# A bias table written in 16 shifted copies, and the scan's decay and angle operands made by ScalarE in pieces

## The chip, the cores and the metric

The kernel runs on one core of a Trainium2 chip. The metric is the device time of one execution in microseconds; the kernel before takes 1424.28 us, the median of three runs (1424.28 to 1425.12).

## The reference, cut to what matters

One decoder block with 256 tokens of width 2048, all in float32. A state-space branch and an attention branch both read the same normed input, are gated and added, and an MLP follows.

```python
mod = c_act @ w_ada[l] + b_ada[l]
...
h = rms_norm(x, norm_mix_g[l]) * (1.0 + sc1) + sh1
proj = h @ w_in[l]
u, q, k, v, ga, gb = jnp.split(proj, split_at, axis=-1)
y_ssm = s5_branch(u, ...)        # diagonal recurrence: 64 groups of 16 channels, 64 complex states
y_att = moba_attention(q, k, v, rel_bias)   # 8 heads, one block of 256 keys: causal softmax
...
merged = (jax.nn.sigmoid(ga) * (y_ssm @ w_proj_ssm[l])
          + jax.nn.sigmoid(gb) * (y_att @ w_proj_attn[l]))
x = x + g1 * (merged @ w_out[l])
h2 = rms_norm(x, norm_mlp_g[l]) * (1.0 + sc2) + sh2
x = x + g2 * (jnp.square(jax.nn.relu(h2 @ w_ff1[l])) @ w_ff2[l])
...
s_own = (jnp.einsum('hqd,hsd->hqs', qc, k_own) * scale
         + bias_table[:, t5_bucket(rel_own)])
s_own = jnp.where(rel_own[None] >= 0, s_own, NEG_INF)
```

The bias of a score depends on the distance of query and key alone (32 buckets, 8 heads). So the table that attention adds is, for each head, one row of 383 numbers that is read at another offset for each query.

## The kernel before, in words

**Weight tiles.** All large products run over one stream of weight tiles of 512 KB (128 x 1024). `load` starts a tile's DMA on SyncE's queue into `wraw` (7 buffers). `split` then makes two parts of it: ScalarE (ACT) casts the high part `whi` (L137) and VectorE (DVE) subtracts it to get the low part `wlo` (L139); each has 4 buffers. TensorE (PE) then runs 24 matmuls for the tile in `gemm_t` (L167 and L168 on `whi`, L169 on `wlo`) or 12 wider ones in `gemm_n` (L219 to L221). Where the text says "tile n", n counts the `wlo` instructions on DVE, in both kernels. A `gemm_t` sums into four banks `pt` of PSUM. Five banks are there for that, so the next product can start on one bank, and needs an evacuation of the last product's banks for each of the others. For the gates of the merge the evacuation is ACT's copy at L1030 into `ga` or `gb`.

**Lanes.** Between the tiles stand small jobs. One lane is the product with `w_ada`, whose tiles go through DVE alone (L275). One makes the state-space operands (`ssm_builds`): complex products `cc` on DVE (`cmul`, L528 to L530), 64 x 64 transposes `trv` (L565) and 128 small matmuls `rk` (L598), which read copies `tt` that ACT spreads (L588) and whose results DVE adds into `rt` (L604). One is attention, head by head: scores `sco` (L652, L653), the bias added by DVE (L655, L656), exponentials and scalings on ACT (L660 to L664), transposes `ptr` (L671) with ACT's copy L672, and values `pav` (L679, L680) with ACT's copy L682. Its scratch lies in columns 8 to 13 of `ga`, the tile that the second half of the first gate is evacuated to; that evacuation waits until the heads are done with the columns. The last lane is the scan.

**The scan.** The 256 tokens are four interleaved blocks b = 0 to 3. For each, `ssm_table` makes sine and cosine of 8 x 64 angles: DVE multiplies `cvec` by `g` (L724), ACT adds and takes off a large constant to round (L726, L727), DVE subtracts (L728), and ACT takes the sine, the absolute value and the sine again (L729, L730, L731). `ssm_in` then runs 32 small matmuls `vr` and `vi` (L745), makes the decay row `dk` on DVE (L747) and rotates the input (L749 to L754). `ssm_scan` is two scan instructions (L762) and six products (L766 to L771), and `ssm_ys` 48 matmuls (L783, L786) and ACT's copy L787.

**The bias.** `bias_prep` multiplies `rel_bias` by a one-hot matrix into 8 rows of 383 and has GpSimd's queue (POOL) write 32 copies of each to DRAM as `scr`. `bias_load` reads them back with four DMAs (L404), each for 32 partitions, so that every partition gets its row at its own offset (`tz`). Ahead of these on POOL's queue stand the 32 DMAs of `hop_in` (L704), which lay `u` out for the scan.

**Who sets the order.** The kernel is built with a planner that simulates the engines and so sets the order of each engine's queue. The text of the program gives the dependences and priorities. When an instruction is taken away, added, or moved to another engine, the planner can order much else in another way. On the chip each engine runs its queue in that order, and an instruction that waits holds all behind it.

Of the kernel before, what the change touches and what calls it, by code (L numbers as in the profile page):

```python
# [12 lines left out]
F32 = mybir.dt.float32  # L13
F32R = mybir.dt.float32r
I32 = mybir.dt.int32
AF = mybir.ActivationFunctionType
# [3 lines left out]
P = 128  # L20
S = 256
# [3 lines left out]
H = 8  # L25
# [13 lines left out]
VL = 383  # L39
# [35 lines left out]
class Kern:  # L75
# [307 lines left out]

    def bias_prep(self):
        nc, a = self.nc, self.a
        both = self.slot("SV", [P, 2, VL], name="oh")
        oh, vec = both[0:32, 0], both[0:H, 1]
        rb = self.cp.tile([32, H], F32, name="rb", tag="rb")
        nc.gpsimd.dma_start(oh, a["onehot"])
        nc.gpsimd.dma_start(rb, a["rel_bias"])  # L390
        p = self.aux("bv")
        with self.after(self.adac):
            nc.tensor.matmul(p[0:H, 0:VL], rb, oh, start=True, stop=True)
        nc.vector.tensor_copy(vec[:, 0:256], p[0:H, 0:256])
        nc.vector.memset(vec[:, 256:VL], NEG)
        self.scr = self.dr.tile([H, 32, VL], F32, name="scr")
        nc.gpsimd.dma_start(self.scr, vec[:, None, :].to_broadcast([H, 32, VL]))

    def bias_load(self):
        self.tz = self.slot("T", [P, H, S], name="tz")  # L400
        s = self.scr
        for g in range(4):
            src = bass.AP(tensor=s.tensor, offset=s.offset + 127 - 32 * g, ap=[[VL - 1, 32], [32 * VL, H], [1, S]])
            self.nc.gpsimd.dma_start(self.tz[32 * g:32 * g + 32], src)  # L404

    def exp_acc(self, x, name):
        nc, v = self.nc, self.nc.vector
# [313 lines left out]
    def ssm_table(self, b):  # L721
        nc, v = self.nc, self.nc.vector
        cs, sn = self.tbl[:, b % 2, 0], self.tbl[:, b % 2, 1]
        v.tensor_mul(sn.rearrange("p (k c) -> p k c", c=64), self.cvec[:, None, :].to_broadcast([P, 8, 64]),  # L724
                     self.g[:, b::4, None].to_broadcast([P, 8, 64]))
        nc.scalar.activation(cs, sn, AF.Identity, bias=self.mpos)  # L726
        nc.scalar.activation(cs, cs, AF.Identity, bias=self.mneg)  # L727
        v.tensor_sub(cs, sn, cs)  # L728
        nc.scalar.activation(sn, cs, AF.Sin, scale=SIN2PI)  # L729
        nc.scalar.activation(cs, cs, AF.Abs)  # L730
        nc.scalar.activation(cs, cs, AF.Sin, scale=-2.0 * math.pi, bias=self.hpi)  # L731
        return cs, sn

    def ssm_in(self, b, tabs):
        nc, v = self.nc, self.nc.vector
        if b + 1 < 4:
            tabs[b + 1] = self.ssm_table(b + 1)
        cs, sn = self.cur = tabs.pop(b)
        pr, pi = self.aux("vr"), self.aux("vi")
        for i, p in ((0, pr), (1, pi)):  # L740
            for k in range(8):
                c = slice(k * 64, (k + 1) * 64)
                for h in range(2):
                    q = slice(64 * h, 64 * h + 64)
                    nc.tensor.matmul(p[q, c], self.VT[q, i, 4 * k + b, :], self.U2[q, b, c], start=True, stop=True)  # L745
        wr, wi, t1, dk = [self.rw[:, i] for i in range(4)]
        v.tensor_mul(dk.rearrange("p (k c) -> p k c", c=64), self.cone[:, None, :].to_broadcast([P, 8, 64]),  # L747
                     self.mag4[:, b::4, None].to_broadcast([P, 8, 64]))
        v.tensor_mul(wr, pr, cs)  # L749
        v.tensor_mul(wi, pr, sn)  # L750
        v.tensor_mul(t1, pi, sn)
        v.tensor_add(wr, wr, t1)
        v.tensor_mul(t1, pi, cs)
        v.tensor_sub(wi, t1, wi)  # L754
# [516 lines left out]
```

## Time and profile before

| | us |
|---|---|
| median of 3 runs | 1424.28 |
| the profiled execution | 1427.57 |
| its span (first to last instruction) | 1425.8 |
| PE busy | 1375.2 |
| DVE busy | 1057.9 |
| ACT busy | 702.3 |
| POOL busy | 38.8 |

A profile is of one execution. Its span is 1.5 us over the median, and its time is 3.3 us over it. Times in rows of the trace count from the start of the span. A row of the timeline has the start, the busy time, engine, line, operation, result and sources, and in brackets the engine's idle time before it with what ended that. Instructions of one engine overlap at their ends, so the distance from one start to the next (here called the pitch) is shorter than a busy time.

### The profile page before, as it was taken

How to read it: one execution, taken by the hardware profiler on the slowest of the kernel's cores; microseconds unless marked ns; L12 is line 12 of the kernel's file. 1: busy time of each engine (PE TensorE's matmuls, PEld its weight loads, DVE VectorE, ACT ScalarE, POOL GpSimd, SP SyncE). 2: the span in 40 equal slices, each digit the busy share in tenths (PEclk: the TensorE clock that was granted, in tenths of full speed). 3: DMA queues.
4: the chain of work that ended last, by engine and by line, in shares of the span. 5: the costliest groups of instructions: out<-in, count | busy, mean ns of one | idle time of the engine just before them, and what ended most of it. 6: DMA issues, size and time to landing. Idle time of an engine off the chain costs nothing.

```text
span 1425.8 us, 23637 instructions
## 1 busy us (share of the span) xinstructions
PE 1375.2 (96%) x9370; PEld 1230.4 (86%) x9370; DVE 1057.9 (74%) x1507; ACT 702.3 (49%) x928; POOL 38.8 (3%) x89
## 2 busy tenths in 40 slices
PE   7789999999999999999899999999999999999996
PEld 5679899999999999988798888888888888888885
DVE  5588989976899788977686685778666555555676
ACT  4345353446645753444555555535364544635444
POOL 1000000310002200000000000000000000000000
PEclk9799999999999999999899999999999999999998
DMA  9999987777557988887497668677767666565561
GB/s 337 332 366 353 333 301 247 239 230 233 159 161 249 316 319 294 292 337 268 169 320 242 196 231 289 222 259 288 253 231 264 178 193 193 176 207 190 180 206 59
DMA packets 114382, 353.41 MB, mean 248 GB/s; under 512 B 12104, under 2 KB 12120, under 8 KB 114144
## 3 DMA queue, kind: packets, MB, share of 16 engines
q1 hardware_dynamic: 111408, 347.13, 71.3%
q0 software_dynamic: 2864, 4.78, 1.3%
q8 instruction: 73, 1.20, 0.3%
q14 instruction: 37, 0.30, 0.1%
HBM read 347.27 MB, written 2.49 MB: 245 GB/s over the span
## 4 chain that ended last, share of the span: by engine, by line
PE 85%; DVE 6%; DMA 4%; issue 2%; ACT 2%; SPq 0%; DVEq 0%; ACTq 0%
PE pw L195 15%; PE pn L221 11%; PE pn L219 11%; PE pn L220 11%; PE pt L169 9%; PE pt L167 9%; PE pt L168 9%; PE pw L197 8%; DVE wraw L275 2%; DMA wraw<-in_w_in_dram 2%; DVE wlo L139 2%; ACT whi L137 1%; DMA wraw<-in_w_proj_attn_dram 1%; PE ss L361 1%; PE rk L598 1%
## 5 line engine op out<-in xcount | busy, mean ns | idle before, releaser
L139 DVE TENSOR_TENSOR wlo<-wraw,whi 128x1024 fp32r<-128x1024 f32 x456 | 553.9, 1223 | 271.3 <-ACT whi L137 269.1
L137 ACT CAST whi<-wraw 128x1024 fp32r<-128x1024 f32 x456 | 474.8, 1050 | 567.4 <-PE pn L220 169.8
L195 PE MATMUL pw<-h2h,whi 128*128 128x512 f32 x960 | 332.8, 396 | 1.0 <-DVE part L1207 0.5
L197 PE MATMUL pw<-h2h,wlo 128*128 128x256 f32 x960 | 259.5, 280 | 1.7 <-DVE wlo L139 1.7
L167 PE MATMUL pt<-ah,whi 128*128 128x256 f32 x896 | 252.4, 289 | 8.0 <-ACT whi L137 5.1
L168 PE MATMUL pt<-ah,whi 128*128 128x256 f32 x896 | 251.8, 286 | 2.4 <-DVE ah L139 2.4
L169 PE MATMUL pt<-ah,wlo 128*128 128x256 f32 x896 | 241.9, 288 | 4.1 <-DVE wlo L139 3.9
L275 DVE SCALAR_TENSOR_TENSOR wraw<-wraw,cb 128x1024 f32<-128x1024 f32 x176 | 213.5, 1219 | 0.0
L195 PEld LDWEIGHTS pw<-h2h,whi 128*128 128x128 f32 x960 | 177.4, 188 | 39.4 <-DVE part L1207 0.8
L220 PE MATMUL pn<-whi,ff 128*128 128x512 f32 x512 | 199.4, 390 | 0.0
L219 PE MATMUL pn<-whi,ff 128*128 128x512 f32 x512 | 198.5, 390 | 0.0
L197 PEld LDWEIGHTS pw<-h2h,wlo 128*128 128x128 f32 x960 | 181.0, 189 | 6.9 <-DVE wlo L139 2.3
L221 PE MATMUL pn<-wlo,ff 128*128 128x512 f32 x512 | 182.7, 390 | 0.0
L167 PEld LDWEIGHTS pt<-ah,whi 128*128 128x128 f32 x896 | 173.0, 194 | 11.3 <-ACT whi L137 6.7
L168 PEld LDWEIGHTS pt<-ah,whi 128*128 128x128 f32 x896 | 173.7, 194 | 3.0 <-DVE ah L139 2.7
L169 PEld LDWEIGHTS pt<-ah,wlo 128*128 128x128 f32 x896 | 166.8, 194 | 5.9 <-DVE wlo L139 5.5
L219 PEld LDWEIGHTS pn<-whi,ff 128*128 128x128 f32 x512 | 96.1, 188 | 20.1 <-issue 0.2
L221 PEld LDWEIGHTS pn<-wlo,ff 128*128 128x128 f32 x512 | 96.1, 188 | 20.0
L220 PEld LDWEIGHTS pn<-whi,ff 128*128 128x128 f32 x512 | 96.1, 188 | 19.6
L219 PE MATMUL pn<-whi,mh 128*128 128x512 f32 x128 | 50.1, 392 | 0.0
L220 PE MATMUL pn<-whi,mh 128*128 128x512 f32 x128 | 49.9, 390 | 0.0
L221 PE MATMUL pn<-wlo,mh 128*128 128x512 f32 x128 | 46.2, 391 | 0.0
(337 smaller groups left out, 1570.5 us busy)
## 6 DMA issues: line engine op xcount, KB each, us to landing
wraw<-in_w_ff_dram SPq DMA_DIRECT2D x256, 512.0 KB, 4.8
wraw<-in_wat_dram SPq DMA_DIRECT2D x176, 512.0 KB, 5.8
wraw<-in_w_in_dram SPq DMA_DIRECT2D x128, 512.0 KB, 5.4
wraw<-in_w_out_dram SPq DMA_DIRECT2D x32, 512.0 KB, 6.5
wraw<-in_wan_dram SPq DMA_DIRECT2D x16, 512.0 KB, 8.9
wraw<-in_w_proj_attn_dram SPq DMA_DIRECT2D x16, 512.0 KB, 7.1
wraw<-in_w_proj_ssm_dram SPq DMA_DIRECT2D x16, 512.0 KB, 5.9
wraw<-in_w_glu_dram SPq DMA_DIRECT2D x8, 512.0 KB, 6.0
```

Of the source, the lines that this page charges most:

```text
L137: h = self.nc.scalar.copy(hi, src)
L139: s = self.nc.vector.tensor_sub(lo, src, hi.bitcast(F32))
L167: nc.tensor.matmul(o, hi[:, c], xh[:, kx, :], start=st, stop=False, skip_group_check=True)
L168: nc.tensor.matmul(o, hi[:, c], xl[:, kx, :], start=False, stop=False, skip_group_check=True)
L169: self.mm = nc.tensor.matmul(o, lo[:, c], xh[:, kx, :], start=False, stop=sp, skip_group_check=True)
L195: nc.tensor.matmul(banks[b], hi[:, c], x2[:, k0 + k].rearrange("p h s -> p (h s)"), start=i + k == 0, stop=False, skip_group_check=True)
L197: self.mm = nc.tensor.matmul(banks[b][:, 0:S], lo[:, c], x2[:, k0 + k, 0, :], start=False, stop=i == n - 1 and k == 1, skip_group_check=True)
L219: nc.tensor.matmul(o, xh[:, kx, tk], hi[:, c], start=q == 0, stop=False)
L220: nc.tensor.matmul(o, xl[:, kx, tk], hi[:, c], start=False, stop=False)
L221: self.mm = last = nc.tensor.matmul(o, xh[:, kx, tk], lo[:, c], start=False, stop=q == n - 1)
L275: v.scalar_tensor_tensor(w, w, 1.0, self.cb[:, (i % 2) * 1024:(i % 2 + 1) * 1024], op0=OP.mult, op1=OP.mult, accum_out=pc[:, i:i + 1])
L361: nc.tensor.matmul(p[:, 0:S], self.ones, jk[:, i, k], start=i + k == 0, stop=i + k == 6)
```

## The change

The diff has three edits. The first writes the bias table from 128 partitions: POOL copies `rel_bias` 16 times side by side, so one matmul gives 128 rows (16 copies of the 8 heads), which one DMA writes as they are. The table in DRAM has 16 copies for each head in place of 32, and `bias_load` reads it with eight DMAs of 16 partitions. The second replaces DVE's product at L724 by eight ACT instructions of 64 columns, each with one column of `g` as its scale. The third does the same for the decay row at L747. Over four blocks that is 8 DVE instructions fewer and 64 ACT instructions more.

```diff
-        both = self.slot("SV", [P, 2, VL], name="oh")
-        oh, vec = both[0:32, 0], both[0:H, 1]
+        both = self.slot("SV", [P, 2 * VL + P], name="oh")
+        oh, vec, rw = both[0:32, 0:VL], both[:, VL:2 * VL], both[0:32, 2 * VL:]
...
+        nc.gpsimd.tensor_copy(rw.rearrange("b (r h) -> b r h", h=H), rb[:, None, :].to_broadcast([32, P // H, H]))
...
-            nc.tensor.matmul(p[0:H, 0:VL], rb, oh, start=True, stop=True)
-        nc.vector.tensor_copy(vec[:, 0:256], p[0:H, 0:256])
+            nc.tensor.matmul(p[:, 0:VL], rw, oh, start=True, stop=True)
+        nc.vector.tensor_copy(vec[:, 0:256], p[:, 0:256])
         nc.vector.memset(vec[:, 256:VL], NEG)
-        self.scr = self.dr.tile([H, 32, VL], F32, name="scr")
-        nc.gpsimd.dma_start(self.scr, vec[:, None, :].to_broadcast([H, 32, VL]))
+        self.scr = self.dr.tile([P, VL], F32, name="scr")
+        nc.gpsimd.dma_start(self.scr, vec)
...
-        for g in range(4):
-            src = bass.AP(tensor=s.tensor, offset=s.offset + 127 - 32 * g, ap=[[VL - 1, 32], [32 * VL, H], [1, S]])
-            self.nc.gpsimd.dma_start(self.tz[32 * g:32 * g + 32], src)
+        for g in range(8):
+            src = bass.AP(tensor=s.tensor, offset=s.offset + 127 - 16 * g, ap=[[H * VL - 1, 16], [VL, H], [1, S]])
+            self.nc.gpsimd.dma_start(self.tz[16 * g:16 * g + 16], src)
...
-        v.tensor_mul(sn.rearrange("p (k c) -> p k c", c=64), self.cvec[:, None, :].to_broadcast([P, 8, 64]),
-                     self.g[:, b::4, None].to_broadcast([P, 8, 64]))
+        for k in range(8):
+            nc.scalar.activation(sn[:, 64 * k:64 * k + 64], self.cvec, AF.Copy,
+                                 scale=self.g[:, 4 * k + b:4 * k + b + 1])
...
-        v.tensor_mul(dk.rearrange("p (k c) -> p k c", c=64), self.cone[:, None, :].to_broadcast([P, 8, 64]),
-                     self.mag4[:, b::4, None].to_broadcast([P, 8, 64]))
+        for k in range(8):
+            nc.scalar.activation(dk[:, 64 * k:64 * k + 64], self.cone, AF.Copy,
+                                 scale=self.mag4[:, 4 * k + b:4 * k + b + 1])
```

With this the planner's order differs between about tile 54 and tile 112; from tile 113 on the queues are alike but for the line numbers (L724 becomes L726 on ACT, L726 to L731 become L728 to L733, L1030 becomes L1033, L598 becomes L599).

**First place: ACT at the start of the scan.** In the kernel before, ACT's queue has this where the tables of blocks 0 and 1 are made and the first gate's banks (`pt_...`) are evacuated:

```order
L137 CAST whi<-wraw 128x1024
L727 ACTIVATE tbl<-tbl,mneg 128x512 x2
L663 ACTIVATE ga<-ga,ast 128x128
L664 ACTIVATE ga<-ga,ast 128x256
L682 COPY yatt<-pav 128x256
L137 CAST whi<-wraw 128x1024
L729 ACT_TABLE_LOAD
L729 ACTIVATE tbl<-tbl 128x512
L1030 COPY ga<-pt_3376 128x512
L729 ACTIVATE tbl<-tbl 128x512
L730 ACTIVATE tbl<-tbl 128x512
L1030 COPY ga<-pt_3377 128x512
```

In the changed kernel, ACT's queue has this at the same place, from the first evacuation on:

```order
L1033 COPY ga<-pt_3384 128x512
L683 COPY yatt<-pav 128x256
L673 COPY ga<-ptr 128x384
L726 ACTIVATE tbl<-cvec,g 128x64 x4
L661 ACTIVATE ga,ast<-ga,ast 128x128
L726 ACTIVATE tbl<-cvec,g 128x64 x4
L662 ACTIVATE ga,ast<-ga,ast 128x256
L726 ACTIVATE tbl<-cvec,g 128x64 x8
L728 ACTIVATE tbl<-tbl,mpos 128x512
L1033 COPY ga<-pt_3381 128x512
L683 COPY yatt<-pav 128x256
L664 ACTIVATE ga<-ga,ast 128x128
```

Sixteen pieces now stand between the first and the second evacuation. The rest of both tables (another L728, two L729, a table load, two L731, two L732) stands ahead of the third, and a cast of a weight tile (tile 101's) only comes after all of it; before, casts, table steps and evacuations took turns.

**Second place: DVE at the same point.** Before, DVE's queue goes from the tables' subtraction over the `wlo` of tiles 99 and 100 to the first block's rotation and scan:

```order
L728 TENSOR_TENSOR tbl<-tbl 128x512 x2
L139 TENSOR_TENSOR wlo<-wraw,whi 128x1024 x2
L747 TENSOR_TENSOR rw<-cone,mag_308 128x512
L749 TENSOR_TENSOR rw<-vr,tbl 128x512
L750 TENSOR_TENSOR rw<-vr,tbl 128x512
L751 TENSOR_TENSOR rw<-vi,tbl 128x512
L752 TENSOR_TENSOR rw<-rw 128x512
L753 TENSOR_TENSOR rw<-vi,tbl 128x512
L762 SCALAR_TENSOR_TENSOR rw<-rw 128x512
```

In the changed kernel the subtraction stands behind the `wlo` of tiles 99 and 100, and DVE's queue goes on from it so:

```order
L730 TENSOR_TENSOR tbl<-tbl 128x512 x2
L139 TENSOR_TENSOR wlo<-wraw,whi 128x1024
L275 SCALAR_TENSOR_TENSOR wraw,pc<-wraw,cb 128x1024
L139 TENSOR_TENSOR wlo<-wraw,whi 128x1024 x2
L752 TENSOR_TENSOR rw<-vr,tbl 128x512
L753 TENSOR_TENSOR rw<-vr,tbl 128x512
L139 TENSOR_TENSOR wlo<-wraw,whi 128x1024
L754 TENSOR_TENSOR rw<-vi,tbl 128x512
```

The three `wlo` ahead of L752 are those of tiles 101, 102 and 103, so the first block's rotation has moved from ahead of tile 101 to behind tile 103.

**Third place: PE at the `rk` matmuls.** Before, they stand in the last product for the keys, in one row (all four blocks of 32):

```order
L598 MATMUL rk<-cc,tt 64x64 x2
L169 MATMUL pt_3049<-ah,wlo 128x256
L167 MATMUL pt_3049<-ah,whi 128x256
L168 MATMUL pt_3049<-ah,whi 128x256
L169 MATMUL pt_3049<-ah,wlo 128x256
L598 MATMUL rk<-cc,tt 64x64 x126
```

In the changed kernel they stand in the last tile of the product for `u`, some tiles earlier, and its matmuls stand between the two pairs of blocks:

```order
L599 MATMUL rk<-cc,tt 64x64 x62
L168 MATMUL pt_2587<-ah,whi 128x256
L169 MATMUL pt_2587<-ah,wlo 128x256
L167 MATMUL pt_2588<-ah,whi 128x256
L168 MATMUL pt_2588<-ah,whi 128x256
L169 MATMUL pt_2588<-ah,wlo 128x256
L167 MATMUL pt_2588<-ah,whi 128x256
L168 MATMUL pt_2588<-ah,whi 128x256
L169 MATMUL pt_2588<-ah,wlo 128x256
L599 MATMUL rk<-cc,tt 64x64 x64
```

The 126 in a row have become 62 and 64, and the DVE products `cc` that they read stand closer ahead of them.

## The prediction

> **What bounds the kernel now.** I read the page's busy shares first, then the chain that ended last:
>
> ```profile
> PE 1375.2 (96%) x9370; PEld 1230.4 (86%) x9370; DVE 1057.9 (74%) x1507; ACT 702.3 (49%) x928; POOL 38.8 (3%) x89
> PE 85%; DVE 6%; DMA 4%; issue 2%; ACT 2%; SPq 0%; DVEq 0%; ACTq 0%
> ```
>
> TensorE is busy 96% of the span and is 85% of the chain. All that the change touches lies beside TensorE, so it can only move the end by what it adds to, or takes from, TensorE's idle time. The order of the queues differs at about tiles 54 to 112, so the next view is TensorE's waits in 250 to 460 us, and after it the table of 20 us windows there (columns: sum, then busy time of PE, PEld, DVE, ACT, POOL):
>
> ```profile
> PE rk L598 <- issue: 2.1, 1, 2.1
> PE pt L169 <- DVE wlo L139: 1.4, 1, 1.4
> ...
> 360.00:380.00 20.00, 20.00 (x261) 19.70 (x260) 13.55 (x20) 15.85 (x26) 0.00 (x0) 1.00 0.44 133
> 380.00:400.00 20.00, 20.00 (x285) 19.60 (x284) 19.96 (x26) 9.05 (x11) 0.00 (x0) 1.00 0.71 227
> 400.00:420.00 20.00, 20.00 (x277) 19.67 (x279) 19.97 (x29) 9.88 (x12) 0.00 (x0) 1.00 0.34 111
> 420.00:440.00 20.00, 18.62 (x236) 18.15 (x232) 19.86 (x28) 7.72 (x10) 0.00 (x0) 1.00 0.63 200
> ```
>
> Only two waits are there to be won: 2.1 us in front of `rk` matmuls and 1.4 us at 431 us. But the windows show a second thing: from 380 to 440 us VectorE is full, 59.8 of 60 us. TensorE lives there on the lead that VectorE had when the scan began, and at 431 us the lead is used up. Whoever starts VectorE's stretch later, or lengthens it, makes TensorE wait; the stretch before it, 360 to 380, is where ScalarE is fullest (15.85 of 20).
>
> **The wait at `rk`.** Three pieces of the chain, then the window behind the wait (the column behind POOL is the granted clock) and the last of ScalarE's spread copies that these matmuls read:
>
> ```profile
> 277.72 5.74 PE rk L598 x191
> 283.46 2.05 issue
> 285.51 3.46 PE rk L598 x61
> ...
> 285.50:290.00 4.50, 4.49 (x70) 4.38 (x70) 1.60 (x4) 0.00 (x0) 3.22 (x7) 0.63 0.40 101
> ...
> 281.47 1.14 ACT L588 COPY tt<-cmp 128x512 f32<-128x512 f32 x2 [0.73 <-PE rk L598]
> ```
>
> The copies end at 282.6, so the 2.05 us from 283.46 are no wait for data ("issue" is a wait that the profile can't name). After it a matmul takes 3.46 / 61 = 0.057 us where it took 5.74 / 191 = 0.030, at a clock of 0.63: 61 x 0.027 = 1.6 us more. In all 3.65 us lie here. The changed order puts 62 and 64 matmuls in two places rather than 126 in one. I don't know whether the wait follows them: the gain is at most 3.65. In the new place VectorE's last `cc` product ends, by my count of its queue, about 0.6 us after TensorE gets there, and a spread copy of 1.14 / 2 = 0.57 us follows: 1.2 us, and 0.3 us for the second pair, so 1.5 us new. Taken: all of the old wait goes and 1.5 us comes, **-2.1 us**; ends -3.65 (nothing new) and +1.5 (old wait follows).
>
> The page "TensorE: Matmul & The Clock Gate" of the Trainium skill (its part on the clock gate) puts the fall of the clock behind an idle window of about 3.4 us; this row has it after 2.05 us, and the row decides. By the page the saving here would be 2.05 us alone.
>
> **The start of the scan, ScalarE.** ScalarE's timeline at the start of the scan before:
>
> ```profile
> 362.20 1.33 ACT L727 ACTIVATE tbl<-tbl,mneg 128x512 f32<-128x512 f32 x2
> 363.44 0.39 ACT L663 ACTIVATE ga<-ga,ast 128x128 f32<-128x128 f32 x1
> 363.74 0.49 ACT L664 ACTIVATE ga<-ga,ast 128x256 f32<-128x256 f32 x1
> 364.14 0.35 ACT L682 COPY yatt<-pav 128x256 f32<-128x256 f32 x1
> 364.55 1.05 ACT L137 CAST whi<-wraw 128x1024 fp32r<-128x1024 f32 x1
> 365.62 1.28 ACT L729 ACT_TABLE_LOAD   x1
> 366.91 0.63 ACT L729 ACTIVATE tbl<-tbl 128x512 f32<-128x512 f32 x1
> 367.45 0.57 ACT L1030 COPY ga<-pt 128x512 f32<-128x512 f32 x1
> 367.91 0.64 ACT L729 ACTIVATE tbl<-tbl 128x512 f32<-128x512 f32 x1
> ```
>
> By pitch: 128 columns 0.30, 256 columns 0.40, so a piece of 64 is estimated at 0.25 (ends 0.20, and 0.33 if columns don't count); 512 columns with a bias 0.62, without 0.54; an evacuation 0.46 to 0.5; the table load 1.28.
>
> Take the end of TensorE's tile 96 as zero. In the new order ScalarE's queue then goes: the first evacuation done at 1.4; the copy of a head's transposes done at 4.3 (it waits for TensorE); 16 pieces, 4.0, with two exponentials between them, 0.9 with their accumulator reads, to 9.2; L728 0.6; the second evacuation done at **10.3**; then a copy, two scalings, L728 and two L729, to 13.15; the load to 14.4; two L731 and two L732, 2.2, to 16.6; the third evacuation done at **17.1**; a sine, a copy, a sine to 18.7; the cast of tile 101 done at **19.65**.
>
> TensorE has tiles 97 to 100 ready but needs banks. By its queue it runs out at 8.3 and waits to 10.3, runs for 3.6 us on the next bank, and waits from 13.9 to 17.1: 2.0 + 3.2 = 5.2 us of idle that were not there before. The pieces make this: without their 4.0 us most of both goes.
>
> The Trainium skill's page "ScalarE: Activation LUTs" (row on a tight latency budget) gives about 0.3 us for an instruction and 0.83 ns for each element, 0.35 for a piece: it speaks against cutting into pieces, and by it the block is 5.6 us and the loss 1.6 larger. This trace's busy times agree (0.39 and 0.49), its pitch doesn't.
>
> **VectorE behind it.** It idles until the table is subtracted, and its full stretch begins with the `wlo` of tile 101 at 19.65. Its prices, from the full stretch:
>
> ```profile
> 429.25 1.21 DVE L762 TENSOR_TENSOR_SCAN rw<-rw 128x512 f32<-128x512 f32 x1
> 430.38 1.20 DVE L139 TENSOR_TENSOR wlo<-wraw,whi 128x1024 fp32r<-128x1024 f32 x1
> 431.50 1.22 DVE L275 SCALAR_TENSOR_TENSOR wraw<-wraw,cb 128x1024 f32<-128x1024 f32 x1
> 432.64 0.08 DVE L275 DVE_READ_ACCUMULATOR wraw<-wraw,cb 128x1 f32 x1
> 432.64 0.69 DVE L754 TENSOR_TENSOR rw<-rw 128x512 f32<-128x512 f32 x1
> 433.25 0.68 DVE L766 TENSOR_TENSOR sri<-rw,tbl 128x504 f32<-128x504 f32 x1
> 433.84 0.68 DVE L769 TENSOR_TENSOR sri<-rw,tbl 128x504 f32<-128x504 f32 x1
> ...
> L747 DVE TENSOR_TENSOR rw<-cone,mag 128x512 f32<-128x512 f32 x4 | 2.7, 686 | 0.3 <-PE pav L680 0.3
> L724 DVE TENSOR_TENSOR tbl<-cvec,g 128x512 f32<-128x512 f32 x4 | 2.6, 683 | 0.0
> ```
>
> A scan is 1.13, a `wlo` 1.14, an L275 1.14, a 512-wide product 0.60. From the `wlo` of tile 101 to that of tile 114 the new queue has 14 `wlo`, 4 L275, 7 scans and 43 products: 16.0 + 4.6 + 7.9 + 25.8 = 54.2 us, so tile 114's `wlo` ends at 19.65 + 54.2 + 0.5 for small gaps = 74.4. The eight products taken off VectorE (2.7 + 2.6 = 5.3 us) are left out already; two of them, for the first two tables, and the first L747 stood in a stretch where VectorE had idle time, and the others shorten the full one.
>
> TensorE's end of tile 96 and its wait for tile 114 before:
>
> ```profile
> 367.55 0.28 PE L169 MATMUL pt<-ah,wlo 128*128 128x256 f32 x1
> 431.63 0.39 PE L169 MATMUL pt<-ah,wlo 128*128 128x256 f32 x1 [1.38 <-DVE wlo L139]
> ...
> 297.12 0.22 PE sco L652 x2
> ```
>
> Between 367.7 and 431.6 it works 63.9 - 1.4 = 62.5 us. In the new order 12 small attention matmuls that stood ahead of tile 96 stand behind it, 12 x 0.22 = 2.6, with changes between forms some 3: 65.5. It waits 74.4 - 65.5 = 8.9 us in all there (5.2 for banks, the rest for `wlo`), against 1.4 before: **+7.5 us**. With pieces at 0.20 it is +6.7, at 0.33 +8.8; if attention's pieces fall better, the bank waits alone are left (below). A slower clock behind the bank waits lies in time that VectorE bounds; behind the last wait it may cost 0 (as after the 1.4 us) to 1.6 us: +0.5.
>
> **The bias and the decay row.**
>
> ```profile
> scr<-oh POOLq DMA_DIRECT2D x1, 383.0 KB, 10.3
> tz<-scr POOLq DMA_DIRECT2D x4, 256.0 KB, 4.8
> L404 POOL DMA_DIRECT2D tz<-scr x4 | 2.4, 597 | 0.0
> ```
>
> The write shrinks to 196 KB: 187 KB less, 0.5 us at the 337 GB/s of the page's first slices if the start is bound by transfers, 0 if not; taken -0.2. Four more issues on POOL are 2.4 us. By the new order `u` is evacuated some 4 us later, `hop_in` ends near 295 and the last `tz` issue near 300, landing near 305. The first head's bias stands four tiles later on VectorE, near 314, so 9 us cover it; without that cover the head, and through the evacuation of `ga` TensorE, would be late by what is missing. The decay pieces, 8 x 0.25 = 2 us on ScalarE for a block, lie where it works 9 of 20 us, and VectorE has five products ahead of the scan that reads them: nothing.
>
> **Sum.** -2.1 + 7.5 + 0.5 - 0.2 = +5.7 us. The profiled execution of 1427.57 would be 1433.3; that is 3.3 us over the median, and taken from the median the forecast is 1424.28 + 5.7 = **1430.0 us**. About 0.2%, 2.85 us, is what a measurement of this kernel can tell from no change.
>
> **Rivals.** *Faster, VectorE relieved.* If a piece's pitch is near 0.1, both evacuations come before TensorE runs out, VectorE's full stretch starts as early as before, its 5 or so products less remove the wait of 1.4 us, and the wait at `rk` goes: -1.4 - 3.65 - 0.5 = -5.5, 1418.8 us. For it: VectorE is the full engine and ScalarE half idle on average. Against it: no pitch in the rows is under 0.30, and ScalarE is not idle at 360 to 380. It decides if the second evacuation ends before 8.3. Chance 0.15.
>
> *No change.* VectorE makes good its late start, so that tile 114's `wlo` ends by 65.5 + 5.2 = 70.7 rather than 74.4 (the order lets it do 3.7 us more before tile 101 than I count). Then the bank waits are left: 5.2 - 1.4 - 3.65 = about 0, 1424.4 us. The bias edit gives nothing by itself in any case, since its cover is there in both. Chance 0.22.
>
> *Slower still.* The unnamed wait comes back in front of the new `rk` rows, with its slow clock, on top of the wait for `cc` (+1.5), and the clock falls behind the wait for tile 114 (+1.6): 7.5 + 1.5 + 1.6 = +10.6, 1434.9 us. For it: half of the 126 matmuls still stand in a row. Chance 0.15. The forecast itself has 0.48.
>
> **Range and chances.** From 1421.5, which leaves out most of the faster case, to 1437, above the slower case with pieces at 0.33. Faster by over 0.2% is the first rival, 0.15; within it is the second, 0.22; slower is the forecast and the third, 0.63.
>
> **What would show it.** In the changed profile: TensorE waits of about 5 us in all for the evacuation at L1033 and some 3 to 4 us for `wlo` between 360 and 445; ScalarE without a gap for about 14 us there; pieces with a pitch of 0.25; VectorE idle for about 10 us ahead of its full stretch; no 2 us of "issue" in `rk`. I am wrong if TensorE stays full from 360 to 420, or if a `rk` wait over 2 us is there.

## The result and the profile after

The changed kernel takes 1438.64 us (median of 4 runs, 1436.25 to 1440.31) against 1424.28 us of the kernel before: the ratio is 1.0083, 95% interval 1.0067 to 1.0099. It is slower, as forecast, but by 14.4 us where 5.7 were forecast, and the time lies 1.6 us above the range. One of the twelve runs of change_slow_lane, further below, took 1936.32 us at a granted clock of 0.653, and the ratios leave it out.

TensorE's waits between 250 and 470 us, in the changed kernel (what waits, for what: us in all, times, longest):

```profile
PE pt L167 <- ACT ga L1033: 5.2, 2, 3.3
PE rk L599 <- ACT tt L589: 3.3, 1, 3.3
PE pt L169 <- DVE wlo L139: 1.3, 1, 1.3
PE pt L167 <- DVE v L905: 1.1, 1, 1.1
PE ys L786 <- DVE sri L771: 0.7, 1, 0.7
```

The waits for the banks are there, two of them, 5.2 us in all. The old unnamed wait at `rk` has gone, and a wait of 3.3 us for ScalarE's spread copies has come. The wait for `v` was not in the forecast. Now the 20 us windows of the changed kernel, as those of before (busy time of PE, PEld, DVE, ACT, POOL, then the granted clock):

```profile
360.00:380.00 20.00, 16.28 (x129) 15.64 (x127) 6.28 (x14) 16.63 (x45) 0.00 (x0) 1.00 0.31 101
380.00:400.00 20.00, 18.53 (x220) 17.84 (x221) 15.07 (x19) 11.95 (x22) 0.00 (x0) 0.83 0.49 168
400.00:420.00 20.00, 19.33 (x274) 18.52 (x272) 19.52 (x27) 13.67 (x35) 0.00 (x0) 1.00 0.55 177
420.00:440.00 20.00, 19.61 (x277) 19.10 (x278) 19.43 (x27) 14.72 (x32) 0.00 (x0) 1.00 0.31 97
```

VectorE works 6.28 of the first 20 us, where it had 13.55 before, and its full stretch starts after 384. In the second window TensorE is busy 18.53 us but runs 220 matmuls where it ran 285: the clock is at 0.83 there.

Waits don't show what a slow clock costs. So the next table takes places at which TensorE has started the same matmuls in each kernel, and gives the time at which the next one starts (read from the traces, one profiled execution each; the kernels from the third column on are experiments, below).

| place | before | after | bias_only | rk_early | bias_slow_lane | change_slow_lane |
|---|---|---|---|---|---|---|
| A, the `pt` matmul behind the first modulation sums | 47.76 | 43.35 | 42.56 | 43.85 | 43.52 | 41.59 |
| B, ahead of the transposes `trv` and of `rk` | 238.77 | 234.36 | 233.73 | 235.84 | 233.94 | 232.88 |
| C, behind `rk` and the last `v` | 314.00 | 313.47 | 310.55 | 313.18 | 307.54 | 306.21 |
| E, the `wlo` of tile 114 | 431.63 | 441.94 | 435.86 | 431.64 | 425.17 | 426.04 |
| F, behind the scan | 485.21 | 495.25 | 489.73 | 486.99 | 477.94 | 479.13 |

Before against after: 4.4 us are won up to A, nothing changes from A to B (191.0 us in both), 3.9 are lost from B to C (75.2 against 79.1), 10.8 from C to E (117.6 against 128.5), and nothing that matters behind E. The traces show some of TensorE's matmuls in another order already from 52 us on, ahead of tile 54; by A to B that costs nothing. In all it is 10.0 us, and the two profiled executions (1437.97 and 1427.57 us) are 10.4 apart. The medians are 14.4 apart, because the profiled execution of before was 3.3 us over its median and that of after 0.7 under it.

### The profile page after: what moved, and what is told of

It is laid out like the page before. It is cut to its first block, busy times and chain, and to the rows that moved or that the text cites. A ratio compares the mean times of both kernels' runs of the same rounds, so it can differ in the third digit from the quotient of the medians.

```text
span 1436.2 us, 23699 instructions
## 1 busy us (share of the span) xinstructions
PE 1379.3 (96%) x9370; PEld 1231.6 (86%) x9370; DVE 1055.1 (73%) x1499; ACT 717.5 (50%) x992; POOL 40.8 (3%) x94
## 4 chain that ended last, share of the span: by engine, by line
PE 84%; DVE 7%; DMA 5%; ACT 3%; issue 1%; SPq 0%; DVEq 0%; ACTq 0%
PE pw L195 15%; PE pn L221 11%; PE pn L219 11%; PE pn L220 11%; PE pt L167 9%; PE pt L169 9%; PE pt L168 9%; PE pw L197 7%; DMA wraw<-in_w_in_dram 2%; DVE wlo L139 2%; DVE wraw L275 2%; ACT whi L137 1%; PE rk L599 1%; DMA wraw<-in_w_ff_dram 1%; PE ss L361 1%
## 5 line engine op out<-in xcount | busy, mean ns | idle before, releaser
L275 DVE SCALAR_TENSOR_TENSOR wraw<-wraw,cb 128x1024 f32<-128x1024 f32 x176 | 213.2, 1218 | 0.0
```

The costliest lines, as they stand in the source:

```text
L275: v.scalar_tensor_tensor(w, w, 1.0, self.cb[:, (i % 2) * 1024:(i % 2 + 1) * 1024], op0=OP.mult, op1=OP.mult, accum_out=pc[:, i:i + 1])
```

## The experiments

Each run was timed beside the kernel before on the same chip. The median of before was 1425.06 us for the first four, 1424.80 for the next four and 1425.48 for the last four.

### Which part of the diff costs what

**bias_only** takes the first edit of the diff alone; the products on VectorE stay. Against the changed kernel:

```diff
-        for k in range(8):
-            nc.scalar.activation(sn[:, 64 * k:64 * k + 64], self.cvec, AF.Copy,
-                                 scale=self.g[:, 4 * k + b:4 * k + b + 1])
+        v.tensor_mul(sn.rearrange("p (k c) -> p k c", c=64), self.cvec[:, None, :].to_broadcast([P, 8, 64]),
+                     self.g[:, b::4, None].to_broadcast([P, 8, 64]))
...
-        for k in range(8):
-            nc.scalar.activation(dk[:, 64 * k:64 * k + 64], self.cone, AF.Copy,
-                                 scale=self.mag4[:, 4 * k + b:4 * k + b + 1])
+        v.tensor_mul(dk.rearrange("p (k c) -> p k c", c=64), self.cone[:, None, :].to_broadcast([P, 8, 64]),
+                     self.mag4[:, b::4, None].to_broadcast([P, 8, 64]))
```

> Only the bias edit; table and decay row stay on VectorE. Theory (two causes): the bias edit's reorder moves the rk matmuls ahead and attention four tiles back, the table pieces make the bank waits. Then this run has the rk wait for the spread copies (about 3.3 us, slow clock behind it) and the wait for v (about 1), bank waits under 1.5 us in all, and takes 1427 to 1431 us. Rival (order alone): all of the loss comes from the reorder, 1437 to 1440 us, with bank waits near 5 us. Rival (pieces alone): 1424 us as before.

Measured: 1434.06 us, ratio 1.0064 (1.0049 to 1.0079). TensorE's waits from 250 to 470 us in this run:

```profile
PE rk L599 <- ACT tt L589: 3.3, 1, 3.3
PE pt L169 <- DVE wlo L139: 2.6, 2, 2.1
PE ys L784 <- DVE sri L769: 1.6, 1, 1.6
PE pt L167 <- DVE v L903: 1.1, 1, 1.1
...
PE pt L167 <- ACT ga L1031: 0.3, 1, 0.3
```

All of the 3.3 and 1.1 us are the bias edit's; the bank waits are not (0.3 us). The time is 3 us over what "two causes" allowed. In the queues of this kernel attention and the tables stand as late as in the changed one (the last head's scores behind tile 100, not 96), so the bias edit alone moved them. I had put that down to the whole diff.

**pieces_only** takes the second and third edits alone:

```diff
-        v.tensor_mul(sn.rearrange("p (k c) -> p k c", c=64), self.cvec[:, None, :].to_broadcast([P, 8, 64]),
-                     self.g[:, b::4, None].to_broadcast([P, 8, 64]))
+        for k in range(8):
+            nc.scalar.activation(sn[:, 64 * k:64 * k + 64], self.cvec, AF.Copy,
+                                 scale=self.g[:, 4 * k + b:4 * k + b + 1])
...
-        v.tensor_mul(dk.rearrange("p (k c) -> p k c", c=64), self.cone[:, None, :].to_broadcast([P, 8, 64]),
-                     self.mag4[:, b::4, None].to_broadcast([P, 8, 64]))
+        for k in range(8):
+            nc.scalar.activation(dk[:, 64 * k:64 * k + 64], self.cone, AF.Copy,
+                                 scale=self.mag4[:, 4 * k + b:4 * k + b + 1])
```

> Only the 64 ScalarE pieces; the bias as before. Two causes: the rk wait is the 2 us of issue of before, the bank waits of the scan's start are there in part (the pieces stand two tiles earlier in ScalarE's queue, with casts between them), 1426 to 1433 us. Rival (order alone): 1424 us. Rival (pieces alone): 1436 to 1440 us.

Measured: 1428.61 us, ratio 1.0027 (1.0015 to 1.0038). No bank wait at all: the same pieces, standing about four tiles earlier (not two, as expected) with casts between them, cost 3.6 us. Where the 3.6 us lie stays open. The profiles don't show it: the queues of the two kernels differ only from 357 us on, and from C to E this one has 118.5 us against 117.6. It is 2.7 us behind at C already (316.67 against 314.00), where the queues are still alike and only the waits and the slow stretches of the clock fell otherwise.

**decay_only** takes the third edit alone:

```diff
-        v.tensor_mul(dk.rearrange("p (k c) -> p k c", c=64), self.cone[:, None, :].to_broadcast([P, 8, 64]),
-                     self.mag4[:, b::4, None].to_broadcast([P, 8, 64]))
+        for k in range(8):
+            nc.scalar.activation(dk[:, 64 * k:64 * k + 64], self.cone, AF.Copy,
+                                 scale=self.mag4[:, 4 * k + b:4 * k + b + 1])
```

> Only the decay row as ScalarE pieces. All theories but one: no change, 1423 to 1426 us. Pieces alone, by their number wherever they stand: half of the loss, 1430 us or more.

Measured: 1424.02 us, ratio 0.9994 (0.9985 to 1.0002), no change. **bias_and_decay** is the changed kernel with the table on VectorE:

```diff
-        for k in range(8):
-            nc.scalar.activation(sn[:, 64 * k:64 * k + 64], self.cvec, AF.Copy,
-                                 scale=self.g[:, 4 * k + b:4 * k + b + 1])
+        v.tensor_mul(sn.rearrange("p (k c) -> p k c", c=64), self.cvec[:, None, :].to_broadcast([P, 8, 64]),
+                     self.g[:, b::4, None].to_broadcast([P, 8, 64]))
```

> Bias edit and decay pieces, the table on VectorE: the changed kernel without the 32 table pieces. Two causes: like the bias edit alone within 1.5 us, 1427 to 1431 us, bank waits under 1.5 us; the rest to 1438.6 is the table pieces'. Order alone: 1437 to 1440 us.

Measured: 1432.84 us, ratio 1.0057 (1.0044 to 1.0069): the bias edit's loss again. So neither rival that names one cause holds, and the decay row is free. Of the 14 us the bias edit makes 8 to 9, the table pieces the rest.

### What the table pieces cost

**one_piece** makes each table's eight pieces one instruction:

```diff
-        for k in range(8):
-            nc.scalar.activation(sn[:, 64 * k:64 * k + 64], self.cvec, AF.Copy,
-                                 scale=self.g[:, 4 * k + b:4 * k + b + 1])
+        nc.scalar.activation(sn.rearrange("p (k c) -> p k c", c=64),
+                             self.cvec[:, None, :].to_broadcast([P, 8, 64]), AF.Copy, scale=self.g[:, b:b + 1])
```

> The changed kernel with each table's eight pieces in one ScalarE instruction of 512 columns; it leaves out that each group of 64 columns has its own scale. If the number of pieces makes the bank waits: they fall from 5.2 to under 2 us, and the time to that of the bias edit with the decay pieces, 1431 to 1434 us. If it is the move from VectorE to ScalarE that costs, whatever the number: bank waits of 4 us or more and 1436 to 1439 us.

Measured: 1431.75 us, ratio 1.0042 (1.0028 to 1.0055), 6.9 us under the changed kernel's median. Its waits from 250 to 470 us are these and no others:

```profile
PE rk L599 <- ACT tt L589: 3.3, 1, 3.3
PE ys L785 <- DVE sri L770: 2.4, 1, 2.4
PE pt L167 <- DVE v L904: 1.1, 1, 1.1
```

The bank waits are gone though ScalarE still makes the table, so the move from VectorE alone doesn't make them: the time is that of bias_and_decay within the noise. The number of pieces and the order aren't separated, though. ScalarE's rows for the second and third evacuation in this run:

```profile
371.81 0.56 ACT L1032 COPY ga<-pt 128x512 f32<-128x512 f32 x1
...
373.78 0.57 ACT L1032 COPY ga<-pt 128x512 f32<-128x512 f32 x1
...
374.74 1.28 ACT L730 ACT_TABLE_LOAD   x1
```

Here the planner put the third evacuation ahead of the table load. In the changed kernel it stands behind the load and four more steps of the tables (380.85, rows further below), none of them a piece, and the longer wait, 3.3 of the 5.2 us, is the one for it. And as each group has its own scale, no run here makes the right table in one instruction.

### What the write costs at the start

**write2_loads4** is the kernel before with the table written from 128 partitions but twice, so that no byte and no load goes away. Against bias_only:

```diff
-        self.scr = self.dr.tile([P, VL], F32, name="scr")
-        nc.gpsimd.dma_start(self.scr, vec)
+        self.scr = self.dr.tile([2, P, VL], F32, name="scr")
+        for i in range(2):
+            nc.gpsimd.dma_start(self.scr[i], vec)
...
-        for g in range(8):
-            src = bass.AP(tensor=s.tensor, offset=s.offset + 127 - 16 * g, ap=[[H * VL - 1, 16], [VL, H], [1, S]])
-            self.nc.gpsimd.dma_start(self.tz[16 * g:16 * g + 16], src)
+        for g in range(4):
+            src = bass.AP(tensor=s.tensor, offset=s.offset + 127 - 32 * g, ap=[[H * VL - 1, 32], [VL, H], [1, S]])
+            self.nc.gpsimd.dma_start(self.tz[32 * g:32 * g + 32], src)
```

> The kernel before with one thing changed: the bias table is written from 128 partitions, in two DMAs of 196 KB, so that as many bytes go as before and the four loads stay; the orders of all engines about the scan, rk and attention are those of before. If the 5 us that TensorE is ahead at 47 us in every profile with the bias edit come from the source's 128 partitions: 1419 to 1421 us, and the wait for the first products' tiles is under 3 us. If they come from the halved bytes: 1423 to 1425 us. If they are chance: 1424 to 1425 us.

Measured: 1422.03 us, ratio 0.9979 (0.9970 to 0.9988): the gain at the start is real, and it doesn't come from the bytes. In the traces TensorE, VectorE and ScalarE run the same instructions in the same order as in the kernel before, so it is no gain of the order either. It is 1 us smaller than expected of the 128 partitions, though the wait for the first tiles falls as expected (below). Queue 0 carries GpSimd's DMAs; of the stretch from 20 to 60 us the DMA view has, in the kernel before, first the moved GB/s in 40 slices of 1 us, then that queue (packets, MB, share of the 16 engines' time):

```profile
GB/s 422 426 393 422 389 422 430 410 410 422 410 283 343 137 87 141 185 51 51 143 334 377 258 303 397 377 336 344 418 410 360 356 352 324 389 373 348 324 299 340
...
q0 software_dynamic: 192, 0.39, 8.5%
```

The same in write2_loads4:

```profile
GB/s 422 410 414 410 385 438 401 410 426 377 385 254 349 320 87 16 180 369 283 238 397 418 401 418 418 418 418 422 406 397 422 406 381 332 258 352 410 356 360 422
...
q0 software_dynamic: 128, 0.39, 2.5%
```

As many bytes take 8.5% of the engines' time from 8 partitions, and 2.5% from 128. All traffic falls to between 51 and 185 GB/s for 7 us before (33 to 40), when the tiles that TensorE waits for should have come, and to between 16 and 180 for 3 us (34 to 37) in write2_loads4. The wait in question, before and in write2_loads4:

```profile
PE adap L247 <- DMA wraw<-in_wan_dram: 5.4, 2, 4.9
```

```profile
PE adap L247 <- DMA wraw<-in_wan_dram: 1.5, 3, 0.6
```

In **write2_pool** GpSimd also makes the angle table:

```diff
-        v.tensor_mul(sn.rearrange("p (k c) -> p k c", c=64), self.cvec[:, None, :].to_broadcast([P, 8, 64]),
+        nc.gpsimd.tensor_mul(sn.rearrange("p (k c) -> p k c", c=64), self.cvec[:, None, :].to_broadcast([P, 8, 64]),
```

> The write from 128 partitions in two DMAs with four loads, and the angle table's product on GpSimd, which is idle there. If VectorE's full stretch is what TensorE waits for at 431 us, taking four products off it without touching ScalarE removes that wait: 1 to 1.5 us under the run with the write alone. If GpSimd and VectorE slow each other down, or the product takes GpSimd too long: the same or slower.

Measured: 1422.49 us, ratio 0.9980 (0.9971 to 0.9989), as without it. The products take 1.1 to 2.0 us each on GpSimd where they took 0.68 on VectorE, and the wait at the end of VectorE's full stretch is still 1.2 us. Taking the table's products off VectorE brings nothing here, though GpSimd has the time.

### What the order costs

**loads8_only** has the eight loads alone, and attention two tiles later in the queues:

```diff
-        for g in range(4):
-            src = bass.AP(tensor=s.tensor, offset=s.offset + 127 - 32 * g, ap=[[VL - 1, 32], [32 * VL, H], [1, S]])
-            self.nc.gpsimd.dma_start(self.tz[32 * g:32 * g + 32], src)
+        for g in range(8):
+            src = bass.AP(tensor=s.tensor, offset=s.offset + 127 - 16 * g, ap=[[VL - 1, 16], [32 * VL, H], [1, S]])
+            self.nc.gpsimd.dma_start(self.tz[16 * g:16 * g + 16], src)
```

> The kernel before with the table read in eight DMAs of 16 partitions; the write stays. Attention moves back by two tiles in the order, rk stays. If a later attention alone costs (VectorE starts its full stretch with less lead): 1426 to 1429 us, with more waits for wlo at 380 to 440 us. If only the rk place and the four tiles of the whole bias edit cost: 1424 to 1425.5 us.

Measured: 1426.04 us, ratio 1.0007 (0.9996 to 1.0018). Eight loads cost nothing that can be told, nor does an attention that begins two tiles later but still ends at tile 96.

**rk_early** is bias_only with four loads. Its queues have `rk` early, as in the changed kernel, but attention ends at tile 97:

```diff
-        for g in range(8):
-            src = bass.AP(tensor=s.tensor, offset=s.offset + 127 - 16 * g, ap=[[H * VL - 1, 16], [VL, H], [1, S]])
+        for g in range(4):
+            src = bass.AP(tensor=s.tensor, offset=s.offset + 127 - 32 * g, ap=[[VL - 1, 32], [H * VL, H], [1, S]])
```

> The bias edit with four loads of 32 partitions from the 16 copies; it leaves out the right offsets, so half of the queries get other biases. The rk matmuls stand early as in the changed kernel, but attention ends at tile 97 rather than 100, and the tables come at tile 97. If the early rk place costs about as much as its gain at the start (3.3 us of wait, 1 us for v, slow clock now and then): 1423 to 1427 us. If rk costs nothing net (the old wait of 3.65 us went): 1419 to 1422 us; then all of the bias edit's loss is attention's lateness. If rk is the whole loss: 1431 us or more.

Measured: 1430.62 us, ratio 1.0039 (1.0027 to 1.0051). That lies between two of the expected ranges: an order with `rk` early costs more than the gain at the start, but isn't the whole loss.

The last three runs change one constant of the planner's input, the rate of the lane that holds the state-space jobs:

```diff
-SR2 = 1.4
+SR2 = 1.1
```

**bias_slow_lane** is bias_only with it.

> The whole bias edit, with one constant more: the lane of state-space jobs runs at 1.1 jobs for a tile in place of 1.4 in its last group. With it the planner puts rk back behind the last keys' tiles, and attention's end and the tables back ahead of tile 97. If the bias edit's loss is the order alone, and its DMA gains at the start: 1419 to 1423 us, no rk wait for the copies. If the smaller write or the eight loads cost by themselves: 1428 us or more.

Measured: 1421.09 us, ratio 0.9967 (0.9955 to 0.9979): 13.0 us under bias_only, with the same DMAs and the same instructions in another order. It isn't the order of the kernel before either. TensorE's waits from 230 to 470 us in it:

```profile
PE pt L169 <- DVE wlo L139: 1.4, 1, 1.4
PE rk L599 <- issue: 0.9, 1, 0.9
```

**change_slow_lane** is the whole change with it.

> The whole change with the same constant. The pieces stay, but stand ahead of tiles 97 and 98 with casts between. If order is all but the pieces' 3 to 4 us of the run with pieces alone: 1423 to 1427 us, bank waits under 1 us. If the pieces cost 7 us wherever they are: 1428 to 1431 us.

Measured: 1423.26 us, ratio 0.9983 (0.9975 to 0.9992). The whole change is 15.4 us faster by this one number, and under the kernel before. ScalarE's timeline at the scan's start in it:

```profile
353.60 0.82 ACT L726 ACTIVATE tbl<-cvec,g 128x64 f32<-128x64 f32 x3
354.33 0.45 ACT L673 COPY ga<-ptr 128x384 f32<-128x384 f32 x1
354.69 1.30 ACT L726 ACTIVATE tbl<-cvec,g 128x64 f32<-128x64 f32 x5
355.89 0.71 ACT L728 ACTIVATE tbl<-tbl,mpos 128x512 f32<-128x512 f32 x1
356.51 1.03 ACT L137 CAST whi<-wraw 128x1024 fp32r<-128x1024 f32 x1
...
360.32 0.56 ACT L1033 COPY ga<-pt 128x512 f32<-128x512 f32 x1
```

The same pieces, but with casts between them and ahead of the first evacuation, so no bank waits for them.

**before_slow_lane** is the kernel before with the constant alone.

> The kernel before with the constant alone, the control for the two runs above. If the constant only serves to choose the order: 1423 to 1426 us. If it gains by itself: 1420 to 1422 us, and the two runs above owe it that.

Measured: 1426.09 us, ratio 1.0004 (0.9995 to 1.0013), no change. So the constant gains nothing by itself; it undoes where the bias edit put `rk` and attention. From 297 us on the queues of before_slow_lane and bias_slow_lane are alike but for one instruction of ScalarE, and with them the bias edit is worth 5.0 us (1426.09 against 1421.09). bias_slow_lane has the lowest median and beats both kernels; its interval overlaps with that of write2_loads4.

## Why the prediction was wrong

**The bank waits were right.** Forecast 2.0 + 3.2 = 5.2 us; measured 5.2 in two waits, the longer 3.3. ScalarE's timeline of the changed kernel has the steps of the walk:

```profile
368.75 1.07 ACT L726 ACTIVATE tbl<-cvec,g 128x64 f32<-128x64 f32 x4
...
371.55 2.00 ACT L726 ACTIVATE tbl<-cvec,g 128x64 f32<-128x64 f32 x8
373.46 0.71 ACT L728 ACTIVATE tbl<-tbl,mpos 128x512 f32<-128x512 f32 x1
374.07 0.56 ACT L1033 COPY ga<-pt 128x512 f32<-128x512 f32 x1
...
377.47 1.28 ACT L731 ACT_TABLE_LOAD   x1
...
380.85 0.56 ACT L1033 COPY ga<-pt 128x512 f32<-128x512 f32 x1
...
382.94 1.04 ACT L137 CAST whi<-wraw 128x1024 fp32r<-128x1024 f32 x1
```

A piece's pitch is 1.91 / 8 = 0.24 (from 371.55 to 373.46), forecast 0.25. The Trainium skill's page "ScalarE: Activation LUTs" has about 0.35 for one instruction of this size (section "Rules for kernel authors", row on a tight latency budget). That agrees with a piece's own busy time here, 0.33; in a queue the pieces overlap by 0.09, and what they pay is the pitch.

**The step that failed in the scan** is VectorE's stretch, "14 `wlo`, 4 L275, 7 scans and 43 products: ... 54.2 us" and "0.5 for small gaps". The stretch has just these instructions, and at tile 114 TensorE waits for VectorE (the 1.3 us above), as forecast:

```profile
384.02 1.22 DVE L139 TENSOR_TENSOR wlo<-wraw,whi 128x1024 fp32r<-128x1024 f32 x1 [5.84 <-ACT whi L137]
...
391.23 0.68 DVE L754 TENSOR_TENSOR rw<-vi,tbl 128x512 f32<-128x512 f32 x1
391.95 0.69 DVE L755 TENSOR_TENSOR rw<-rw 128x512 f32<-128x512 f32 x1
...
395.11 1.23 DVE L139 TENSOR_TENSOR wlo<-wraw,whi 128x1024 fp32r<-128x1024 f32 x1 [0.61 <-ACT whi L137]
...
440.69 1.20 DVE L139 TENSOR_TENSOR wlo<-wraw,whi 128x1024 fp32r<-128x1024 f32 x1
```

It starts 19.4 us behind TensorE's end of tile 96 (364.6), where 19.65 were forecast, but takes 57.9 us, not 54.7. Of the 3.2 us, 1.4 are waits for casts and for `vr`, and both wait for TensorE. The rest is the pitch: fifteen times an instruction that needs the one just ahead of it to be done starts some 0.12 us later than others do (391.23 to 391.95 is 0.72, and the sum took 0.60 for all 43 products). So tile 114's `wlo` ends 77.3 us behind tile 96 rather than 74.4. With attention's matmuls at 2.5 us rather than 3 that makes 10.8 from C to E where 7.5 were forecast. TensorE's waits between the two are 7.6 us where 8.9 were forecast: 5.2 for the banks, 1.3 for `wlo` rather than 3.7, and 1.1 for `sri`.

The wait for `wlo` is short because TensorE was late itself: it took 69.7 us for what the forecast had at 65.5. The clause "a slower clock behind the bank waits lies in time that VectorE bounds" priced that at nothing. Two matmuls of the chain, which runs through TensorE there:

```profile
382.05 0.21 PE pt L168
...
390.22 0.12 PE pt L169
```

A matmul that takes 0.12 takes 0.21, for some 5.5 us behind the longer bank wait: 5.5 x 0.09 / 0.21 = 2.4 us more of TensorE's time. What of it reached tile 114's `wlo` is at most the 1.4 us that VectorE waited, so but for those the clause holds. The 0.5 us that the sum has for the clock stood for the last wait, and the clock didn't fall there.

**The step that failed at `rk`** is "1.2 us, and 0.3 us for the second pair". The chain there:

```profile
259.21 1.23 DVE cc L531
260.47 0.63 ACT tt L589
261.14 0.48 PE rk L599 x4
261.62 0.51 PE pt L169
262.13 0.21 PE pt L167
262.35 6.20 PE rk L599 x124
```

The mechanism was the forecast one: VectorE's last `cc` product, the copy, the matmuls. But TensorE gets there 2.6 us before the `cc` product ends rather than 0.6, and waits 3.3 us; and behind the wait the clock is low, 6.20 / 124 = 0.050 us for a matmul against 0.030. From B to C it cost 3.9 us, not -2.1, the wait for `v` (1.1 us) among them. bias_only has the same two waits without the low clock, and takes 76.8 us from B to C against 79.1: the low clock is some 2.3 of the 3.9. A wait over 2 us at `rk` was the prediction's own sign of being wrong.

**The bias edit, -0.2 us**, was the third miss, on the other side: 3.4 to 6.2 us are won up to A in each of the nine profiles that have the write from 128 partitions (the changed kernel's 4.4 among them), and 0.9 us at most in the four others. I priced the write by its bytes. The Trainium skill's page "DMA: Bandwidth & Descriptors" says (section "Rules for kernel authors") that a slowest dimension smaller than 16 confines a whole DMA to as many engines. By that page the write from 8 partitions would keep to 8 of the 16. The trace agrees: in the kernel before, from 37 to 39 us, nothing but queue 0 moves, and it holds half of the engines' time:

```profile
q0 software_dynamic: 23, 0.10, 49.0%
```

Why the same bytes also take 3.4 times as much of the engines' time in all (8.5% against 2.5%) stays open. The row that should have led there was in the prediction's own fence: 10.3 us to land 383 KB, when a tile of 512 KB takes 5.4.

**What the sum left out altogether** is that order is a cause of its own. The forecast priced the edits at their new places. bias_slow_lane and change_slow_lane show that the edits aren't bound to those places: in an order with `rk` behind the last keys' tiles and attention ending at tile 96, the bias edit gains 4.4 us and the whole change 2.2. Split by each run's distance from the kernel before beside it, from bias_slow_lane (-4.4) on: the order with `rk` early costs 9.5 us (rk_early, +5.1), the late attention with its tables 3.9 more (bias_only, +9.0), the table pieces in that place 5.4 more (the changed kernel, +14.4); together 18.8. These are names of orders, each of which moves more than one thing. Of the 9.5, the table of places shows 1.6 from A to B, where the queues are alike and only the waits and the clock fell otherwise, 3.7 from B to C, which is `rk`, 0.8 from C to E and 2.6 from E to F. The scan stands in another order there too, and from E to F two waits are new in rk_early:

```profile
PE pt L167 <- ACT gb L1031: 1.2, 1, 1.2
PE ys L784 <- DVE sri L772: 1.1, 1, 1.1
```

So the traces put 3.7 us on `rk` itself; how much of the rest follows from it is not shown. Why the planner puts `rk` early when the write is smaller was not looked into: rk_early has it with one write, write2_loads4 not with two.

Of the rivals, the third (a slower clock behind the new waits, 1434.9 us) came nearest: a new wait at `rk` with its slow clock. The wait was for data, not the unnamed one, and the clock didn't fall behind the wait for tile 114, which was its other half.

## What to carry to other kernels

When a planner sets the order, price an edit twice: by what its instructions cost, and by what the order does with the rest; then try the edit with the moved jobs put back before it is judged. Behind each wait of TensorE of about 2 us and more, look at the granted clock, and count the matmuls that it slows if TensorE is the bound there. In a sum of many small instructions, those that need the one just ahead have a pitch of their own. A DMA is priced by how many partitions it comes from as well as by its bytes; a long time to landing in the profile shows it.

## What the runs showed of the hardware

The clock's fall behind a wait is a matter of the wait's place as well as of its length. The windows behind the 3.3 us at `rk` and behind the longer bank wait, in the changed kernel (the granted clock is the number behind POOL):

```profile
261.00:267.60 6.60, 6.46 (x106) 6.12 (x108) 5.79 (x9) 3.73 (x7) 0.00 (x0) 0.50 0.69 204
380.40:387.00 6.60, 5.53 (x25) 5.53 (x26) 2.98 (x4) 5.89 (x10) 0.00 (x0) 0.50 0.09 28
```

The window behind the same wait at `rk` in bias_only:

```profile
261.00:267.60 6.60, 6.60 (x184) 6.26 (x185) 6.49 (x11) 5.24 (x8) 0.00 (x0) 1.00 0.74 231
```

106 matmuls there, 184 here, behind the same wait. Over all runs, by the granted clock in the traces: behind the wait of 3.3 us at `rk` it fell in four of five profiles (the changed kernel, one_piece, bias_and_decay, rk_early; not in bias_only), each time for 6.8 us at half. Behind the unnamed wait of 2.0 to 2.3 us it fell in three of six (before, pieces_only, write2_pool), for 3.4 us. Behind the waits of 0.7 to 1.0 us of the three slow-lane runs it never did.

The traces show what the place means. Every slow stretch in them, but for the one that runs past the end, lasts whole steps of 3.41 us (3.41, 6.83, 10.24 and so on), and within a trace they start whole steps apart: in the kernel before at 22.58, 39.65, 169.35 and 285.41 us, that is 5, 38 and 34 steps. So there is one grid of 3.41 us in a trace, and it lies otherwise in the next run. Over the 14 traces, from 70 to 680 us: behind each of the 15 steps at full clock in which TensorE idled 1.89 us or more, the next step is slow; behind none with 1.54 or less; and behind two of the five between. It is the idle time within one step that counts. The 3.3 us at `rk` lie with 2.97 in one step in the changed kernel, and with 1.74 and 1.51 in two steps in bias_only; the 2.1 us of the kernel before with 1.95 in one step, those of decay_only with 0.81 and 1.33 in two.
